# A hybrid attention and MLP step on one core: new tables for the order of loads, splits and joins around a ring of 53 tiles

## The chip, the cores and the metric

The kernel runs on one core of one Trainium2 chip. The metric is the device time of one execution in microseconds; the times given are medians of several runs. Engines are named as in the profile: PE (TensorE, with PEld for its weight loads), DVE (VectorE), ACT (ScalarE), POOL (GpSimd) and SP (SyncE, here only the issuer of transfers).

## The reference, cut to what matters

Two streams of 128 tokens (`prompt` and `sample`, width 2048) go through one layer with the same weights, in float32:

```
shift1, scale1, gate1, shift2, scale2, gate2 = split(silu(c) @ w_ada + b_ada, 6)
h  = rms_norm(x, norm1_w) * (1 + scale1) + shift1
qA, kA, vA, qB, kB, vB, gA, gB = split(h @ w_in)          # 2048 x 8704
oA = windowed GQA (8 heads, 2 key heads, sink), oB = neighbourhood attention (8 heads)
     # sample queries also see cached context keys
x  = x + gate1 * ((sigmoid(gA) * (oA @ w_br_a) + sigmoid(gB) * (oB @ w_br_b)) @ w_out)
h2 = rms_norm(x, norm2_w) * (1 + scale2) + shift2
y  = x + gate2 * (relu(h2 @ w_up) ** 2 @ w_down)          # 2048 x 8192 and back
```

The outputs are `y` of both streams and the new keys and values of the prompt.

## The kernel before, in words

**Products.** Each float32 product is made of three products of fp32r halves: high by high, low by high, high by low. A weight tile `raw` (128x1024, 512 KB) is loaded by SP (L243); ACT copies its high half `wH` (`copy`, L112; `prep_hi`); DVE subtracts to get the low half `wL` (`prep`, L272). Then PE does a *step*: 12 matmuls of 128x512, for two k-tiles, two streams and three products (`mm3`, L347 to L349; `start_steps`, L474 to L476 in the in-projection). A few low halves are made by a transfer instead (`minus_plus`, L278, L279: ACT writes minus the high half, and a POOL transfer adds the weight to it); the table `LO_DMA` says which.

**Ring.** All 128x1024 tiles, weights and activations alike, come from one ring of `GEN` = 53 buffers (`G`, L95). A load can only be issued when the buffer that it takes is free.

**Order.** The program is one list of some 460 weight steps. `run` (L314) goes through it once. At step i it emits the loads that are due up to `RUN[i]` steps ahead, the splits (high and low half) up to `LOOK[i]` steps ahead, further high halves up to `AHEAD[i]` steps, then the step's matmuls, and behind them whatever other work is hung at that step: `at(i, ...)` and `ex(i, ...)` for instructions, `load_at(i, ...)` for loads. Nothing is reordered later: each engine and each queue takes its work in the order in which it was emitted. So tables of step numbers set everything.

**Work hung between the steps**, as far as the change and the prediction speak of it:

- *Modulation blocks.* `pair_load` (L356) loads four tiles `araw` of w_ada, and `pair_mm` (L365) puts one block of 16 narrow matmuls (128x256, accumulator `ps_ada`) on PE. `ADA_AT` and `ADA_LD` place those of sub-layer 1 and their loads, `SS_AT` those of the first part of sub-layer 2: six blocks `fb` = 0 to 5, each at the step that the table gives for it. Blocks at the same step follow each other without a weight matmul between them. The other modulation columns are dot products on DVE (`aT`, L1685; `DOTS`, `DOTS1`, `DOTS2` place them).
- *Attention.* `att_job` (L896) makes seven pieces for each of eight items (mixer, stream s, group g); `JOBS` places them. The probabilities must be transposed. Items in `TE` do that on PE: `probs_T` (L964), four 128x128 transposes into the accumulator `ps_PT` (L970), and one ACT copy to `PT`. All other items do it by a transfer: `probs_part` (L973) has ACT write the two 16-bit planes `plPA`, `flip` (L1059) has SP issue a DMA_TRANSPOSE to `pTPA` (L1062), and `join_full` (L1065) has ACT put the planes together as `fTPA`. For an item of the prompt stream (s = 0) the tiles are half as large.
- *Pairs of w_up pieces.* The 16 pieces of w_up go in eight pairs. The first pair is plain; the others go through `up_pair` (L1409), which has eight positions. A position listed in `FAST` is done by seven products of sums instead of eight: two tiles (`x`, `y`), 21 matmuls (L1419 to L1421), and on DVE a *group* of seven operations: `t` (L1506), `XL` (L1510), a sum (L1511), `YB` (L1513), a sum (L1514), `tL` (L1516) and `uL` (L1517). The other positions are plain: two tiles, 24 matmuls, two `wL` on DVE. `XL_DMA` and `YL_DMA` name the positions whose `XL` or `YB` low half is made by a POOL transfer instead (index 8 times pair plus position), and `T_DMA` those whose sums are made early.
- *Down units.* Behind each pair follow four units of w_down; their sums are carried from pair to pair in a ring tile `dsum`. `DS_AWAY` lists those that wait in DRAM instead (`ds`, one 512 KB transfer out and one back each). `AWAY` lists gate tiles that do the same, and `G2_LEAD` says how many steps before the end of a last down unit its gate and its old residual are fetched.

Of the kernel before, what the change touches and what calls it, by code (L numbers as in the profile page):

```python
# [33 lines left out]
SILU_AT = 6  # L34
FB_DVE = 6
FB1 = 14
H_AT = 38
DOTS1 = [20, 27, 30, 34, 34, 34, 38, 42]
# [30 lines left out]
ADA_AT = [None, 5, 14, 16, 22, 34, 40]
XS_AT = {1: 5, 2: 12, 3: 36}  # L70
POST = {('kvA', 0): [66, 70, 73], ('qA', 0): [66, 69, 75, 75, 77], ('qA', 1): [70, 75, 75, 82, 82], ('kB', 0): [75, 77, 79, 80, 82], ('qB', 0): [81, 82, 86, 88, 90], ('kB', 1): [84, 86, 91, 92, 95], ('qB', 1): [85, 92, 99, 100, 100]}
JOBS = [[80, 80, 81, 85, 88, 89, 92], [82, 83, 84, 86, 90, 97, 104], [83, 86, 86, 89, 90, 90, 105], [89, 91, 92, 93, 93, 105, 109], [95, 95, 98, 100, 100, 102, 114], [95, 101, 102, 104, 107, 111, 116], [106, 106, 108, 108, 121, 123, 127], [108, 111, 116, 117, 117, 120, 124]]
# [18 lines left out]
def tile_hybrid_step(ctx: ExitStack, tc: tile.TileContext, a):  # L91
# [143 lines left out]
    def add_step(src, mm, key, half=0, xkey=None, tkey=None):  # L235
# [660 lines left out]
    def att_job(mix, s, g):  # L896
# [512 lines left out]
    def up_pair(p):  # L1409
# [32 lines left out]
        for pos, is_fast in enumerate(kinds):  # L1442
# [37 lines left out]
            def prep_y(b=b, pos=pos):  # L1480
                if "t" in b:
# [378 lines left out]
```

## Time and profile before

| | |
|---|---|
| median of 3 runs | 1313.43 us (1312.73 to 1314.02) |
| the profiled execution | 1312.65 us |
| its span in the profile | 1310.8 us |
| granted TensorE clock | 0.999 of full |
| PE, DVE, ACT, POOL busy | 99%, 86%, 69%, 4% of the span |
| moved by DMA | 400.9 MB, mean 306 GB/s |

The span is the profile's own time from the first to the last recorded event; the execution's time is 1.85 us longer. Busy time is time in which an engine had an instruction under way. Because PE overlaps its matmuls, a row's own duration (0.39 us for a 128x512 matmul) is longer than the distance from one start to the next, and it is the distance that adds up.

### The profile page before, as it was taken

To read this page: it belongs to the slowest core of one execution; us is meant where nothing else is said; L and a number is where in the kernel's file an instruction comes from. 1 tells how busy PE (TensorE), PEld (TensorE's weight loads), DVE (VectorE), ACT (ScalarE), POOL (GpSimd) and SP (SyncE) were. 2 spreads that over 40 slices of the span, in tenths; PEclk is the share of its full clock that TensorE was granted. 3 is DMA by queue.
4 is the path that set the end of the run, shared out by engine and by line. 5 is a ranking of instruction groups with operands and counts; after the bars stand their busy time and mean duration, and the time that the engine had idled before them with its cause. 6 is when DMAs were issued, how large, how long until landed. Compare 5 with 4: busy or idle time off the path is not lost.

```text
span 1310.8 us, 17957 instructions
## 1 busy us (share of the span) xinstructions
PE 1303.2 (99%) x6333; PEld 1057.9 (81%) x6334; DVE 1126.5 (86%) x1446; ACT 904.5 (69%) x1145; POOL 57.4 (4%) x66
## 2 busy tenths in 40 slices
PE   9999999999999999999999999999999999999998
PEld 4778788788788878888888888888888888888887
DVE  4669799989999899999778998987999998789663
ACT  5635566699865655636786878859779597696980
POOL 0000000332000000000000000000000000000000
PEclk9999999999999999999999999999999999999999
DMA  9999999897999989997599789779977978869593
GB/s 371 408 409 408 400 409 389 346 321 232 271 347 349 386 294 365 359 334 235 205 300 318 204 269 287 275 269 273 322 240 238 362 245 278 301 205 367 193 355 96
DMA packets 170138, 400.90 MB, mean 306 GB/s; under 512 B 71840, under 2 KB 73088, under 8 KB 170048
## 3 DMA queue, kind: packets, MB, share of 16 engines
q1 hardware_dynamic: 165744, 387.36, 82.3%
q0 software_dynamic: 4160, 12.32, 5.0%
q8 instruction: 49, 0.80, 0.2%
q14 instruction: 41, 0.34, 0.1%
q10 hardware_dynamic: 144, 0.08, 0.1%
HBM read 373.97 MB, written 10.80 MB: 294 GB/s over the span
## 4 chain that ended last, share of the span: by engine, by line
PE 98%; ACT 1%; DMA 1%; SPq 0%; issue 0%; DVE 0%; ACTq 0%
PE acc L347 17%; PE acc L348 17%; PE acc L349 17%; PE Q L1421 6%; PE Q L1420 6%; PE Q L1419 6%; PE acc L474 5%; PE acc L475 5%; PE acc L476 5%; PE ps_ada L365 3%; PE ps_S L920 1%; PE Z L1421 1%; PE Z L1420 1%; PE Z L1419 1%; DMA araw<-in_w_pair 1%; PE acc L1225 1%
## 5 line engine op out<-in xcount | busy, mean ns | idle before, releaser
L272 DVE TENSOR_TENSOR wL<-raw,wH 128x1024 fp32r<-128x1024 f32 x377 | 442.7, 1219 | 51.2 <-ACT wH L112 49.0
L112 ACT ACTIVATE wH<-raw 128x1024 fp32r<-128x1024 f32 (+1 forms) x394 | 388.5, 1039 | 62.3 <-DMA raw<-in_w_in 22.6
L474 PE MATMUL acc<-wH,hH 128*128 128x512 f32 x272 | 107.1, 394 | 0.6 <-ACT srow L112 0.6
L475 PE MATMUL acc<-wL,hH 128*128 128x512 f32 x272 | 105.9, 389 | 0.0
L476 PE MATMUL acc<-wH,hL 128*128 128x512 f32 x272 | 105.9, 389 | 0.0
L347 PE MATMUL acc<-wH,hH 128*128 128x512 f32 x252 | 101.2, 402 | 0.0
L348 PE MATMUL acc<-wL,hH 128*128 128x512 f32 x252 | 98.3, 390 | 0.0
L349 PE MATMUL acc<-wH,hL 128*128 128x512 f32 x252 | 98.2, 390 | 0.0
L1685 DVE CUSTOM_DVE_ANT_0 aT<-aT,cB,cols 128x1024 f32<-128x1024 f32 x56 | 71.4, 1283 | 0.6
L1685 DVE CUSTOM_DVE_ANT_0 junk<-aT,cB,cols 128x1024 bf16<-128x1024 f32 x56 | 71.2, 1279 | 0.0
L112 ACT ACTIVATE uH<-raw 128x1024 fp32r<-128x1024 f32 x34 | 36.1, 1062 | 47.4 <-DVE raw L1514 38.2
L474 PEld LDWEIGHTS acc<-wH,hH 128*128 128x128 f32 x272 | 51.0, 188 | 14.2 <-issue 2.9
L476 PEld LDWEIGHTS acc<-wH,hL 128*128 128x128 f32 x272 | 51.1, 188 | 10.8
L475 PEld LDWEIGHTS acc<-wL,hH 128*128 128x128 f32 x272 | 51.1, 188 | 10.2
L347 PEld LDWEIGHTS acc<-wH,hH 128*128 128x128 f32 x252 | 47.4, 188 | 10.6 <-issue 1.0
L348 PEld LDWEIGHTS acc<-wL,hH 128*128 128x128 f32 x252 | 47.4, 188 | 10.5 <-issue 0.7
L349 PEld LDWEIGHTS acc<-wH,hL 128*128 128x128 f32 x252 | 47.3, 188 | 9.9
L112 ACT ACTIVATE tH<-t 128x1024 fp32r<-128x1024 f32 x31 | 32.8, 1058 | 30.4 <-DVE t L1506 26.2
L112 ACT ACTIVATE fTa<-pTa 128x2048 uint16<-128x2048 uint16 x16 | 40.5, 2533 | 1.3 <-DVE gc_g L1685 1.3
L1685 DVE CUSTOM_DVE_ANT_0 aT<-aT,cB,gc_g 128x1024 f32<-128x1024 f32 x32 | 40.7, 1282 | 0.4
L1685 DVE CUSTOM_DVE_ANT_0 junk<-aT,cB,gc_g 128x1024 bf16<-128x1024 f32 x32 | 40.7, 1280 | 0.0
L1562 ACT ACTIVATE up<-up 128x1024 f32<-128x1024 f32 x28 | 29.7, 1062 | 15.4 <-DVE up L1552 14.9
(694 smaller groups left out, 3351.9 us busy)
## 6 DMA issues: line engine op xcount, KB each, us to landing
raw<-in_w_in SPq DMA_DIRECT2D x131, 512.0 KB, 9.0
raw<-in_w_down SPq DMA_DIRECT2D x128, 512.0 KB, 6.8
araw<-in_w_pair SPq DMA_DIRECT2D x80, 512.0 KB, 9.8
raw<-in_w_upF SPq DMA_DIRECT2D x68, 512.0 KB, 6.3
aT<-in_w_gT SPq DMA_DIRECT2D x64, 512.0 KB, 7.1
raw<-in_w_up SPq DMA_DIRECT2D x60, 512.0 KB, 6.8
aT<-in_w_adaT SPq DMA_DIRECT2D x48, 512.0 KB, 8.0
raw<-in_w_out SPq DMA_DIRECT2D x32, 512.0 KB, 7.8
```

The lines of the kernel that those rows point to most:

```text
L112: act.activation(out, in_, AF.Copy)
L272: dve.tensor_tensor(st["lo"], st["raw"], st["hi"].bitcast(F32), op=OP.subtract)
L347: pe.matmul(acc[tb], sh, wh[:, k, :], start=f, stop=False, **kw)
L348: pe.matmul(acc[tb], sh, wl[:, k, :], start=False, stop=False, **kw)
L349: pe.matmul(acc[tb], sl, wh[:, k, :], start=False, stop=l, **kw)
L474: pe.matmul(acc[tb], sh, wh[:, k, :], start=kt == 0 and k == 0 and not held and not seeded, stop=False, **kw)
L475: pe.matmul(acc[tb], sh, wl[:, k, :], start=False, stop=False, **kw)
L476: pe.matmul(acc[tb], sl, wh[:, k, :], start=False, stop=last and k == 1 and not hold, **kw)
L1419: pe.matmul(acc, stat[0], hi, start=f, stop=False)
L1420: pe.matmul(acc, stat[0], lo, start=False, stop=False)
L1421: pe.matmul(acc, stat[1], hi, start=False, stop=l)
L1685: dve.tensor_tensor_reduce(out, box["raw"], cB[s, tag], 1.0, dst if second else baT[:, part, fb:fb + 1], OP.mult, OP.add, dst)
```

## The change

Only tables change; the functions are the same. In the new tables:

- `SS_AT` puts the six modulation blocks of sub-layer 2 at steps 49, 73 (three) and 140 (two) instead of 53 (two), 73 (two), 125 and 141.
- `TE` no longer lists item ('A', 0, 1): its probabilities go by a transfer.
- `FAST` has seven-product groups at other positions in pairs 1, 2, 4, 5 and 7; the number in each pair is the same. Pair 7 now has three in a row (2, 3, 4).
- `XL_DMA` now makes 6 `XL` by transfer instead of 10, `YL_DMA` 8 `YB` instead of 7, `LO_DMA` 11 low halves instead of 7.
- `DS_AWAY` parks 5 down sums instead of 8; `AWAY` parks one gate instead of two.
- `G2_LEAD` fetches the last gates and residuals three steps later, and `ADA_LD` the modulation tiles of sub-layer 1 up to three steps earlier.
- `LOOK`, `RUN`, `AHEAD` and the tables that place the other work (`DOTS`, `POST`, `JOBS`, `T_PAIR`, `P_PAIR` and more) are new throughout.

```
-H_AT = 38
...
+H_AT = 26
...
-TE = (('A', 0, 1), ('qA', 1), ('qB', 1))
-DS_AWAY = [8, 9, 12, 15, 19, 21, 22, 23]
+TE = (('qA', 1), ('qB', 1))
+DS_AWAY = [16, 19, 21, 22, 23]
 DS_BACK = 6
-YL_DMA = [8, 9, 15, 23, 29, 31, 39]
-T_DMA = {15: 10, 48: 10, 55: 7}
+YL_DMA = [8, 9, 15, 16, 23, 29, 31, 63]
+T_DMA = {15: 10, 48: 11, 55: 7}
 G2_PARTS = 1
 PREP_LATE = 9
-G2_LEAD = 2
-ADA_LD = [1, 1, 0, 2, 0, 0, 0]
+G2_LEAD = -1
+ADA_LD = [2, 1, 3, 2, 0, 0, 0]
 BEGIN_SEED = ()
-FAST = {1: (0, 1, 5, 7), 2: (0, 2, 3, 5, 7), 3: (0, 2, 3, 5, 7), 4: (0, 1, 3, 6, 7), 5: (0, 1, 3, 5, 7), 6: (0, 1, 3, 5, 7), 7: (0, 1, 3, 5, 7)}
-AWAY = [('gB', 0), ('gB', 3)]
-GATE_BACK = 3
...
+FAST = {1: (0, 1, 3, 7), 2: (0, 2, 4, 5, 7), 3: (0, 2, 3, 5, 7), 4: (0, 1, 3, 5, 7), 5: (0, 1, 3, 4, 7), 6: (0, 1, 3, 5, 7), 7: (0, 2, 3, 4, 7)}
+AWAY = [('gB', 3)]
+GATE_BACK = 0
...
-LO_DMA = {186: 8, 205: 8, 218: 9, 357: 6, 402: 6, 448: 7, 455: 3}
...
+LO_DMA = {157: 10, 184: 10, 204: 8, 285: 8, 320: 7, 328: 7, 350: 3, 351: 7, 402: 10, 452: 10, 454: 5}
...
-XL_DMA = {9: 8, 16: 10, 21: 7, 23: 9, 26: 7, 35: 9, 38: 11, 43: 9, 55: 10, 61: 8}
...
+XL_DMA = {9: 8, 16: 8, 19: 5, 21: 7, 23: 9, 38: 10, 43: 9, 55: 10, 61: 10, 62: 9}
...
-SS_AT = [53, 53, 73, 73, 125, 141]
+SS_AT = [49, 73, 73, 73, 140, 140]
```

(An index in `XL_DMA` that stands at a plain position has no effect.) Three places show how the order moves. In the rows below, numbers behind a name are those of a buffer's use and differ between the two programs.

**PE, in the products with w_br_a and w_br_b.** `acc` is a weight unit's accumulator; `ps_ada<-araw,cpad` is a modulation block. The trace counts two records to each of its matmuls, so x16 here is x32 in the rows of the trace. Before, the last two blocks of `SS_AT` stood apart, in two places:

```order
L348 MATMUL acc<-wL,hH_1159 128x512
L349 MATMUL acc<-wH,hL_1160 128x512
L365 MATMUL ps_ada<-araw,cpad 32x256 x16
L347 MATMUL acc<-wH,hH_1698 128x512
L348 MATMUL acc<-wL,hH_1698 128x512
...
L348 MATMUL acc<-wL,oHB_3839 128x512
L349 MATMUL acc<-wH,oLB_3840 128x512
L365 MATMUL ps_ada<-araw,cpad 32x256 x16
L347 MATMUL acc<-wH,oHB_4147 128x512
L348 MATMUL acc<-wL,oHB_4147 128x512
```

Now:

```order
L348 MATMUL acc<-wL,oHB_3883 128x512
L349 MATMUL acc<-wH,oLB_3884 128x512
L365 MATMUL ps_ada<-araw,cpad 32x256 x32
L347 MATMUL acc<-wH,oHB_3883 128x512
L348 MATMUL acc<-wL,oHB_3883 128x512
```

The two are one block of 32. Of the other four, which were 32 and 32 in two places, one now stands alone earlier (16) and three together (48). In all there are nine blocks behind the first 47 us where there were ten.

**ACT, in the attention stage**, around the item that leaves PE. `plPA` and `fTPA` are the item's planes and their join, `PT` the copy of what PE transposed, `plqB`, `fTqB` and `plkB` those of other tiles. Before:

```order
L112 ACTIVATE wH<-raw 128x1024 x3
L112 ACTIVATE fTPA_3120<-pTPA_3090 128x2x512
L112 ACTIVATE wH<-raw 128x1024 x2
L112 ACTIVATE fTqB_3153<-pTqB_3088 128x2x1024
L857 ACTIVATE fTqB_3153<-fTqB_3153,cols 128x1024
L112 ACTIVATE PT<-ps_PT 128x512
L112 ACTIVATE plkB_3195<-u_kB_2300 128x1024 x2
```

Now:

```order
L112 ACTIVATE wH<-raw 128x1024
L112 ACTIVATE fTPA_3120<-pTPA_3031 128x2x512
L112 ACTIVATE plPA_3122<-prob 128x512 x2
L112 ACTIVATE wH<-raw 128x1024 x4
L112 ACTIVATE fTqB_3154<-pTqB_3118 128x2x1024
L857 ACTIVATE fTqB_3154<-fTqB_3154,cols 128x1024
L112 ACTIVATE fTPA_3161<-pTPA_3159 128x2x512
L945 ACTIVATE prob,den<-ps_S,nm 128x256 x4
L951 ACTIVATE es<-es 128x4
L112 ACTIVATE plkB_3207<-u_kB_2335 128x1024 x2
```

`PT` is gone; two `plPA` and one `fTPA` have come. On SP the item's transpose is the fourth in a row, ahead of the next weight load; before, three stood there.

**DVE, in pair 7 of w_up**, from the end of one group on. Before, two `wL` of a plain position stood between groups:

```order
L1516 TENSOR_TENSOR tL<-t_10815,tH 128x1024
L1517 TENSOR_TENSOR uL<-raw,uH 128x1024
L272 TENSOR_TENSOR wL<-raw,wH 128x1024 x2
L1506 TENSOR_TENSOR t_10898<-raw 128x1024
L1511 TENSOR_TENSOR raw<-t_10898,raw 128x512
```

Now three groups follow each other:

```order
L1516 TENSOR_TENSOR tL<-t_10729,tH 128x1024
L1517 TENSOR_TENSOR uL<-raw,uH 128x1024
L1506 TENSOR_TENSOR t_10760<-raw 128x1024
L1510 TENSOR_TENSOR XL<-raw,XH 128x1024
L1511 TENSOR_TENSOR raw<-t_10760,raw 128x512
L1513 TENSOR_TENSOR YB<-raw,YB 128x512
L1514 TENSOR_TENSOR raw<-raw 128x512
L1516 TENSOR_TENSOR tL<-t_10760,tH 128x1024
L1517 TENSOR_TENSOR uL<-raw,uH 128x1024
L1506 TENSOR_TENSOR t_10805<-raw 128x1024
```

The third group is full, with its `XL` on DVE; a block of four `wL` stands behind it.

## Rows read from the trace of the kernel before

**Rows 1.** The page, part 1: busy time and share of the span, instructions.

```profile
PE 1303.2 (99%) x6333; PEld 1057.9 (81%) x6334; DVE 1126.5 (86%) x1446; ACT 904.5 (69%) x1145; POOL 57.4 (4%) x66
```

**Rows 2.** The page, part 4: the chain that ended last, by engine.

```profile
PE 98%; ACT 1%; DMA 1%; SPq 0%; issue 0%; DVE 0%; ACTq 0%
```

**Rows 3.** Waits of PE: line waited for, us in total, times, longest.

```profile
PE ps_warm L136 <- DVE wm L129: 1.2, 1, 1.2
```

**Rows 4.** Timeline of PE at 308 us: start, us, engine, line, tiles, shapes.

```profile
308.31 0.39 PE L349 MATMUL acc<-wH,hL 128*128 128x512 f32 x1
...
309.67 0.39 PE L349 MATMUL acc<-wH,hL 128*128 128x512 f32 x1
309.90 0.60 PE L970 MATMUL ps_PT<-ident,prob 128*128 128x128 f32 x4
...
310.80 0.40 PE L349 MATMUL acc<-wH,hL 128*128 128x512 f32 x1
```

**Rows 5.** Timeline of PE at 194 us: a joined block.

```profile
194.04 0.39 PE L476 MATMUL acc<-wH,hL 128*128 128x512 f32 x1
194.36 3.66 PE L365 MATMUL ps_ada<-araw,cpad 128*32 128x256 f32 x64
...
198.52 0.39 PE L476 MATMUL acc<-wH,hL 128*128 128x512 f32 x1
```

**Rows 6.** Timeline of PE at 421 us: a block that stands alone.

```profile
421.50 0.39 PE L349 MATMUL acc<-wH,hL 128*128 128x512 f32 x1
421.82 1.93 PE L365 MATMUL ps_ada<-araw,cpad 128*32 128x256 f32 x32
...
424.26 0.39 PE L349 MATMUL acc<-wH,hL 128*128 128x512 f32 x1
```

**Rows 7.** Timeline of PE at 268 us.

```profile
268.03 0.39 PE L347 MATMUL acc<-wH,hH 128*128 128x512 f32 x1
...
268.62 0.39 PE L349 MATMUL acc<-wH,hL 128*128 128x512 f32 x1
```

**Rows 8.** Timeline of DVE at 267 us.

```profile
267.03 3.48 DVE L272 TENSOR_TENSOR wL<-raw,wH 128x1024 fp32r<-128x1024 f32 x3
```

**Rows 9.** Windows: us, busy PE, PEld, DVE, ACT, POOL, clock, DMA share, GB/s.

```profile
30.00:60.00 30.00, 29.36 (x180) 22.75 (x179) 20.55 (x28) 21.09 (x33) 0.00 (x0) 1.00 1.03 408
300.00:330.00 30.00, 30.00 (x154) 25.21 (x153) 27.16 (x42) 28.92 (x51) 3.66 (x3) 1.00 0.76 199
1170.00:1200.00 30.00, 30.00 (x135) 24.82 (x134) 29.25 (x30) 21.57 (x28) 0.87 (x1) 1.00 0.89 316
```

**Rows 10.** Timeline of ACT, 294 to 320 us: pieces of attention items.

```profile
296.21 1.15 ACT L112 ACTIVATE plPA<-prob 128x512 uint16<-128x512 uint16 x2
...
311.02 1.40 ACT L112 ACTIVATE fTPA<-pTPA 128x1024 uint16<-128x1024 uint16 x1
...
317.78 0.58 ACT L112 ACTIVATE PT<-ps_PT 128x512 f32<-128x512 f32 x1
```

**Rows 11.** Timeline of SP's queue at 302 us: transposes.

```profile
302.31 12.55 SPq L1062 DMA_TRANSPOSE pTPA<-plPA  x2
```

**Rows 12.** Timeline of DVE, 1170 to 1181 us: a group, start to start.

```profile
1170.32 1.23 DVE L116 TENSOR_TENSOR a13L<-fTa,a13H 128x1024 fp32r<-128x1024 f32 x1 [3.72 <-ACT a13H L112]
1171.46 2.35 DVE L272 TENSOR_TENSOR wL<-raw,wH 128x1024 fp32r<-128x1024 f32 x2
1173.73 1.22 DVE L1506 TENSOR_TENSOR t<-raw 128x1024 f32<-128x1024 f32 x1
...
1180.29 1.22 DVE L1506 TENSOR_TENSOR t<-raw 128x1024 f32<-128x1024 f32 x1
```

**Rows 13.** Timeline of PE at 1179 us: the first product of pair 7.

```profile
1179.36 0.39 PE L1419 MATMUL Q<-XH,h20H 128*128 128x512 f32 x1
```

**Rows 14.** Timeline of PE at 71 us: behind a modulation block.

```profile
71.32 0.50 PE L474 MATMUL acc<-wH,hH 128*128 128x512 f32 x1
```

**Rows 15.** Timeline of SP's queue at 1286 us.

```profile
1286.28 0.34 SPq L1583 DMA_DIRECT2D out_y_prompt<-x1b  x1
```

More of the change, by code (lines that the diff above doesn't have):

```diff
@@ L36 @@
 FB1 = 14
-H_AT = 38
-DOTS1 = [20, 27, 30, 34, 34, 34, 38, 42]
+H_AT = 26
+DOTS1 = [18, 28, 31, 34, 34, 35, 38, 42]
 CHUNKS = [2, 2, 2, 4, 6]
@@ L56 @@
-AWAY = [('gB', 0), ('gB', 3)]
-GATE_BACK = 3
-SEED_IN = {3: -1, 4: -1}
+FAST = {1: (0, 1, 3, 7), 2: (0, 2, 4, 5, 7), 3: (0, 2, 3, 5, 7), 4: (0, 1, 3, 5, 7), 5: (0, 1, 3, 4, 7), 6: (0, 1, 3, 5, 7), 7: (0, 2, 3, 4, 7)}
+AWAY = [('gB', 3)]
+GATE_BACK = 0
+SEED_IN = {3: -1, 4: 0}
 SEED_AT = 4
 DIRECT = (3,)
-LO_DMA = {186: 8, 205: 8, 218: 9, 357: 6, 402: 6, 448: 7, 455: 3}
-LOOK = "320000020500002000113432224544355446105343223385524450433655335345220455511216541254444406744443240165443463136211143544456397555524342453545433224531546677753453557412434789853455586466303567898461134235331776545653214545433434534422123768733734502102522243854523655760005645555536452367642004332333245620031043144643220323340312252125324443413423321411333333446345833326123111223423654523544524557100124130023323212212653354124352222546524348984222137443"
@@ L66 @@
-CONST_AT = [73, 75]
-XL_DMA = {9: 8, 16: 10, 21: 7, 23: 9, 26: 7, 35: 9, 38: 11, 43: 9, 55: 10, 61: 8}
+LO_DMA = {157: 10, 184: 10, 204: 8, 285: 8, 320: 7, 328: 7, 350: 3, 351: 7, 402: 10, 452: 10, 454: 5}
+LOOK = "321120021500113212223432223344442225005343223375534342423655446345220456622316541254444404744443240065433351036222042434453289545523232344667633114531546677653453557645534688853485586468513567897361134235333996534653214524222446767643234766513734512102532243864523655860003644655325231155424223132323346742242243144542222302340312252126324443413423322633442234456355833327123111223422543623544502557200224130023545242212653354110142222546412236685233237443"
@@ new lines @@
+RUN = "878887888999967489774426566652243043332113515655542236844445543454663225725104564635347113386421231025420310432200023642333255530101233552468375724663533896686664869999999999799967677624674845057865762774435787755674676471011155366289975888700001010012023644555422226413232357543567947344664412222454243314331337774655600562333412455543455532421531552123100023944336934475787876510000441302144625845546341022443004889667656654243123677999787767425666774210"
+AHEAD = "221111000000000000000000000000000000000000122113121111111211101011122221001010133110000100000333100021133111112211133200001011244001000000000111001111010000000000000010111000111000000000121244220100020000000002320000000003022411110111110002000002111345442330002136444661455741000000000011000003100000002220000000000000000120000010000000001000200111223363222222000000000010000020000000013322222200011112223422222123000202100001100200013121123545251212345402"
@@ L68 @@
+CONST_AT = [66, 71]
+XL_DMA = {9: 8, 16: 8, 19: 5, 21: 7, 23: 9, 38: 10, 43: 9, 55: 10, 61: 10, 62: 9}
 ADA_G = ((1,), (2,), (3, 4), (5, 6))
[L69 to L72, printed above, removed]
+ADA_AT = [None, 5, 14, 16, 22, 35, 40]
@@ new lines @@
+XS_AT = {1: 3, 2: 14, 3: 40}
+POST = {('kvA', 0): [66, 70, 73], ('qA', 0): [64, 69, 74, 76, 78], ('qA', 1): [70, 75, 75, 82, 82], ('kB', 0): [73, 77, 79, 81, 83], ('qB', 0): [78, 82, 86, 89, 90], ('kB', 1): [84, 86, 91, 93, 98], ('qB', 1): [86, 97, 98, 100, 100]}
+JOBS = [[80, 80, 83, 85, 86, 89, 93], [82, 83, 84, 86, 90, 94, 106], [83, 86, 86, 89, 90, 90, 103], [86, 90, 92, 93, 93, 105, 109], [94, 94, 101, 102, 102, 106, 116], [96, 103, 104, 106, 109, 109, 115], [106, 107, 108, 108, 118, 122, 127], [109, 111, 114, 117, 119, 122, 126]]
@@ L73 @@
 SS_G = [(0, 2), (2, 1)]
-SS_AT = [53, 53, 73, 73, 125, 141]
+SS_AT = [49, 73, 73, 73, 140, 140]
 T_AT = [3, 4]
-PREP_IN = [4, 7]
-DOTS = [37, 45, 46, 50, 50, 51, 52, 54, 56, 56, 56, 57, 61, 63, 65, 67, 70, 73, 77, 84, 89, 91, 92, 93, 96, 97, 102, 103, 104, 106, 108, 109, 109, 112, 114, 117, 118, 120, 122, 122, 123, 126, 129, 129, 129, 132, 133, 137, 138, 138, 140, 144, 145, 146, 156, 156, 156, 160, 160, 163, 167, 169, 173, 173, 175, 175, 178, 179, 179, 182, 182, 183]
-DOTS2 = [225, 231, 234, 235, 237, 238, 245, 245, 258, 266, 268, 270, 270, 294, 300, 301, 306, 327, 328, 331, 333, 336, 349, 359, 360, 362, 363, 367, 394, 395, 396, 401]
@@ L79 @@
-STAT_AT = [2, -1, 9, 1]
-T_PAIR = [[14, 4], [6, 9], [8, 8], [5, 8], [8, 9], [5, 10], [6, 12]]
-P_PAIR = [[5, -1], [1, 1], [0, 5], [1, 5], [1, 6], [0, 5], [3, 0]]
+PREP_IN = [6, 7]
+DOTS = [30, 46, 49, 50, 50, 52, 54, 54, 56, 56, 56, 56, 57, 62, 64, 67, 70, 73, 77, 84, 89, 91, 92, 93, 96, 97, 102, 103, 104, 106, 108, 109, 109, 112, 114, 117, 118, 120, 122, 122, 123, 126, 129, 129, 129, 132, 133, 137, 138, 138, 140, 144, 145, 148, 155, 156, 157, 160, 161, 163, 167, 169, 173, 173, 175, 175, 178, 179, 179, 182, 183, 188]
@@ L82 @@
+DOTS2 = [222, 231, 233, 234, 237, 238, 245, 245, 264, 266, 268, 270, 270, 291, 300, 301, 304, 327, 328, 331, 333, 336, 349, 359, 360, 362, 363, 367, 392, 395, 396, 401]
+STAT_AT = [6, 2, 9, 11]
+T_PAIR = [[14, 4], [5, 9], [10, 8], [5, 8], [9, 7], [8, 10], [12, 12]]
+P_PAIR = [[5, -1], [1, 2], [1, 4], [2, 3], [0, 2], [4, 5], [2, 1]]
 M_TE = (3,)
-M_AT = [1, 2, 6]
+M_AT = [1, 2, 8]
 FLIP = 1
-P_UP = [4, 2]
-T_UP = [13, 11]
+P_UP = [5, 3]
+T_UP = [13, 10]
 COL = {"qA": 0, "kvA": 1024, "qB": 1536, "kB": 2560, "vB": 3584, "gA": 4608, "gB": 6656}
```

2 lines of the change are left out of this document (removed).

## The prediction

> **What bounds the kernel now.** I read four views, in this order. The page's busy times say that PE has an instruction under way for 1303.2 of 1310.8 us [rows 1]; only 7.6 us of the span are left. The chain that ended last says the same from the other side: 98% of it is PE, nothing else has more than 1% [rows 2]. So the time is the sum of what stands in PE's queue, unless something makes PE wait. The view of PE's waits has five entries; the largest is 1.2 us [rows 3], and all five belong to the start, before weight products run without a break. Last I read PE's timeline for the distance from one weight matmul to the next: from 308.31 to 309.67 there are six, 1.36 / 6 = 0.227 us each [rows 4]. A row's own 0.39 us is overlapped and may not be added up. A step of 12 matmuls is thus 2.72 us.
>
> DVE at 86% and ACT at 69% [rows 1] are off the path on average, but not everywhere: ACT is busy for 28.92 of 30 us in the attention stage from 300 us, DVE for 29.25 of 30 in w_up's last pair from 1170 us [rows 9]. There a change of order can turn into a wait of PE.
>
> The profiled execution took 1312.65 us, 0.78 below the median of 1313.43. I form the sum against the execution and carry the difference over to the median.
>
> **The change part by part.**
>
> *The attention item that leaves PE.* Its four transposes stand in PE's queue between two weight matmuls whose starts are 1.13 us apart (309.67 to 310.80), with three weight distances in that stretch: 1.13 - 0.68 = 0.45 us [rows 4]. This goes: **-0.45 us**. In exchange ACT makes two plane copies (1.15 together) and a join (1.40) and saves a copy (0.58): +1.97 us [rows 10], where it has 1.08 us idle in 30 [rows 9]. SP gets a fourth transpose in a row; two of them, with their waits, held its queue for 12.55 us [rows 11], so one more is worth 0 to 6.3 us to the loads behind it. Neither is on the path as long as splits and loads are ahead of PE. The new tables let loads be issued up to eight steps (22 us) and splits four (11 us) ahead there. I take 0 and keep +1.97 us, the whole ACT time, as the upper end.
>
> *The joined modulation blocks.* A block of 32 (x64 in the trace's count) stretches the distance around it from 3 x 0.227 = 0.68 to 4.48 us: it costs 3.80 [rows 5]. One of 16 (x32) costs 2.76 - 0.68 = 2.08 [rows 6]. Two apart are 4.16, together 3.80; each separate block costs 0.36 us for its being separate. PE's order has nine blocks behind the first 47 us and had ten: **-0.36 us**. The block of 48 and the single one of 16 are priced by the same split of 1.72 us per 16 matmuls plus 0.36, so only the count of blocks matters. Bounds: 0 if the fixed part is that of neighbours that stay, 0.72 if two joins count.
>
> *A small hitch at 268 us.* Two starts that should be 0.45 us apart are 0.59 apart [rows 7]: PE's low-half product waited for the first `wL` of three, which began at 267.03 behind a block of DVE work on a query tile and ended 1.2 us later [rows 8]. In the new order that `wL` stands ahead of the query's work. **-0.14 us**, with 0 as the other end.
>
> *Seven-product groups in other places.* The number of groups is the same, so PE has the same weight matmuls (5382 in both orders). What moves is DVE's work. A group takes 1180.29 - 1173.73 = 6.56 us on DVE [rows 12], while PE needs 21 x 0.227 = 4.77 us for it: DVE falls back 1.79 us per group. A plain position is 2.27 us on DVE (1171.46 to 1173.73) against 24 x 0.227 = 5.45 on PE: DVE gains 3.18. Pair 7 now has three groups in a row, all with `XL` on DVE. I lay them out from the row at 1170.32: group 0 begins at 1173.73 and ends at 1180.29; two `wL` end at 1182.56; the groups at positions 2, 3 and 4 begin at 1182.56, 1189.12 and 1195.68. The last one's `tL` ends one `uL` earlier than the group (1.14): 1201.10. PE starts the pair at 1179.36 [rows 13] and reaches the first product with that `tL` after 21 + 24 + 21 + 21 + 6 + 4 = 97 matmuls: 1179.36 + 97 x 0.227 = 1201.38. That is **0.3 us in time**. I take 0; the other end is the slower rival.
>
> *Low halves moved between DVE and transfers.* Four more `XL` on DVE and one fewer `YB`, two fewer `wL`: about +2 us of DVE in 1310, and -2 us of ACT's negated copies. Away from pair 7 this is covered by DVE's 14% of idle time; I take 0, and without that cover it is counted in pair 7 already.
>
> *Fewer parked tiles, other loads.* Three down sums and a gate no longer go out and back: eight transfers of 512 KB less. At the full rate of 408 GB/s such a tile takes 1.285 us [rows 9], but PE waits for no load behind the start, so it gains 0. In the first 60 us the transfers are the scarce thing (share 1.03, [rows 9]). There the modulation tiles of f = 2 now pass weight tiles. In SP's new order 46 tiles of 512 KB go out up to the weights of step 17: 46 x 1.285 = 59.1 us, some 62 with the start. The first product behind the block at that place begins at 71.32 [rows 14]. 9 us in hand; 0, at the other end about 1 us if splits queue up too. At the end, the last gate and residual are now fetched behind the output at 1286.28 [rows 15], some 13 us before the last unit's first half needs them, ten times a tile's 1.285 us: 0.
>
> **Sum:** -0.45 - 0.36 - 0.14 = **-0.95 us**. The profiled execution would take 1311.7, the median 1313.43 - 0.95 = **1312.5 us**. That is 0.07%, below the 0.2% (2.6 us) which a measurement of this kernel can tell from no change.
>
> [...] The trace shows the four transposes at 0.45 us of PE and their replacement at 1.97 us of ACT plus a transfer. [...]
>
> **The rivals.**
>
> 1. *ACT runs out of lead in the attention stage.* Place: 300 to 330 us. For it: ACT is busy for 28.92 of 30 us there. Against it: PE waited for no high half in that stretch before, although ACT was as full. Price: up to the whole 1.97 us, so 1312.5 + 1.97 = 1314.5.
> 2. *The join does not do what it says.* The words speak of two joins, but the order has only one block less, and the other regrouping splits one pair to make a three. If a block's fixed price lies in work that stays, or small hitches of that size come up elsewhere, only the transposes count: 1313.43 - 0.45 = 1313.0.
> 3. *Slower: DVE misses pair 7.* One mechanism: three groups in a row with no `XL` by transfer. Its margin by the rows is 0.3 us, and its start hangs on an ACT copy for which DVE had idled 3.72 us [rows 12]. Each us beyond the margin is a us of PE, since nothing later gives PE idle time back. The upper price is the fall-back of all three, 3 x 1.79 = 5.4 us: 1312.5 + 5.4 = 1317.9. It decides the sign by the 0.2% when DVE starts the pair 3.9 us later than in the trace (0.3 of margin, then 2.63 + 0.95 of wait). Against it: DVE's idle 3.72 us lie just ahead of the pair, so a part of them is a cushion if the copy comes sooner.
> 4. *Faster by over 0.2%.* Even with all five waits of the start gone, the 7.6 us outside PE's busy time are mostly warm-up, first loads and the tail, which the tables don't touch. I find no place for 2.6 us.
>
> **How the numbers follow.** Forecast 0.62 (1311.6 to 1313.2 by its own bounds); rival 1 has 0.15, rival 2 0.11, rival 3 0.08 and rival 4 0.04. Rivals 1 and 2 lie within 0.2% of 1313.43, so *same* has 0.62 + 0.15 + 0.11 = 0.88, *slower* 0.08, *faster* 0.04. The range: down by the second join's 0.36 and the spread of runs below the median (0.70) from 1312.5, 1311.4; up to rival 1's 1314.5 and the spread above (0.59), 1315.0 rounded. Rivals 3 and 4 are left out, 12 in 100.
>
> **What would show it.** In the changed profile: rows of L970 gone; a x64 block in the merge products and a x96 one earlier, with distances of about 4.5 and 6.2 us around them; PE's weight distance still 0.227; PE's busy time and the span about 1 us lower; PE's waits still those of the start. Rival 1 would show as distances over 0.23 us at high-half products (L347, L474) between 300 and 340 us; rival 3 as a gap of PE ahead of an L1420 with `tL` near 1200 us, behind DVE that has no idle time from 1170 on. The forecast is wrong if the span moves by more than 2 us, or if the time moves by 1 us in rows that I priced at nothing.

## The result, and the profile after

| | before | the change |
|---|---|---|
| median of the runs | 1313.36 us (7 runs, 1312.48 to 1314.02) | 1316.50 us (7 runs, 1315.75 to 1318.93) |
| ratio | | 1.0030 (95%: 1.0019 to 1.0042) |
| profiled execution, its span | 1312.65, 1310.8 us | 1315.75, 1314.0 us |

The change made the kernel slower by 3.1 us where 0.95 us less had been forecast, and its executions spread over 3.2 us, those of the kernel before over 1.5. The page's busy times and chain of the changed kernel, which answer to [rows 1, 2]:

```profile
PE 1302.9 (99%) x6330; PEld 1057.4 (80%) x6330; DVE 1129.1 (86%) x1447; ACT 906.1 (69%) x1147; POOL 56.4 (4%) x65
...
PE 96%; DMA 3%; ACT 1%; SPq 0%; issue 0%; DVE 0%; ACTq 0%
```

PE is busy for 0.3 us less, but the span is 3.2 us longer: what came is waiting, and the chain says for what. DMA has 3% of it, three times as much as before. The view of PE's waits names the tile:

```profile
PE ps_ada L365 <- DMA araw<-in_w_pair: 3.1, 4, 1.0
```

This line is new; the next largest wait is that of [rows 3]. PE waits four times for tiles of modulation weights. PE's timeline shows where; first the one at the start, in the changed kernel, and then the other three, inside the joined block of 48 matmuls (x96 in the trace's count, here in pieces x72, x8, x8 and x8):

```profile
20.37 0.64 PE L365 MATMUL ps_ada<-araw,cpad 128*32 128x256 f32 x8 [0.99 <-DMA araw<-in_w_pair]
...
251.86 4.09 PE L365 MATMUL ps_ada<-araw,cpad 128*32 128x256 f32 x72
256.47 0.64 PE L365 MATMUL ps_ada<-araw,cpad 128*32 128x256 f32 x8 [0.52 <-DMA araw<-in_w_pair]
257.75 0.64 PE L365 MATMUL ps_ada<-araw,cpad 128*32 128x256 f32 x8 [0.64 <-DMA araw<-in_w_pair]
259.39 0.64 PE L365 MATMUL ps_ada<-araw,cpad 128*32 128x256 f32 x8 [1.00 <-DMA araw<-in_w_pair]
259.96 0.66 PE L869 MATMUL ps_qT<-ident,u_kvA 128*128 128x128 f32 x4
```

The three pieces of x8 are 1.3 to 1.6 us apart. That is about the pace of the transfers (1.285 us for 512 KB at 408 GB/s, [rows 9]), not of PE, which does a piece in 0.43 us (1.72 us per 16 matmuls). From the block's first start to that of `ps_qT` it takes 8.10 us. A block of 32 at this place takes 3.59 us (253.67 to 257.26 in the trace of e2 below), and 16 matmuls more are 1.72: 5.31. (In e4 below, where the same block of 48 doesn't wait, it takes 5.32.) So **2.79 us are waiting**. The bracketed idle times add up to less (2.16), because each row's own 0.64 us overlaps. SP's queue in the same trace says why the tiles are late:

```profile
234.17 14.40 SPq L356 DMA_DIRECT2D araw<-in_w_pair  x12
```

And in the kernel before:

```profile
234.10 8.49 SPq L356 DMA_DIRECT2D araw<-in_w_pair  x8
```

The burst of modulation tiles begins at the same time in both, but it has twelve tiles instead of eight. Twelve take 14.40 us to issue, at the full rate of the transfers, and the last lands 10.8 us after its issue (248.57 to 259.39). The burst did not begin sooner because SP was held up at the loads that stand ahead of it in its queue: between 200 and 230 us it waits once for 7.9 us until PE (L476) and once for 3.8 us until DVE (L272) has used a tile, that is, for free ring buffers. The windows of the changed kernel show it as transfers that stand idle (the columns are those of [rows 9]):

```profile
200.00:230.00 30.00, 30.00 (x134) 24.83 (x133) 29.96 (x45) 20.16 (x29) 0.00 (x0) 1.00 0.71 263
230.00:260.00 30.00, 27.85 (x194) 20.59 (x192) 28.97 (x43) 14.49 (x25) 19.05 (x17) 1.00 1.03 410
```

First 263 GB/s, then 410 and no more to be had. But waits for buffers are only a part of the idle time. From 216.3 to 218.5 us SP issues five small loads of constants (`rope` with 128 KB, three `cpad` with 64 KB each, `sink` with 4 KB), and while these are under way the transfers crawl; `sink` with its 4 KB takes 8.9 us from issue to landing. Loads of 512 KB had been issued behind them by then (`cbv`, at 220.05, takes 10.2 us to land). In the kernel before the same five stand shortly ahead of the burst. First a window of the changed kernel, then one of the kernel before:

```profile
218.00:227.00 9.00, 9.00 (x41) 7.48 (x40) 8.96 (x13) 6.87 (x11) 0.00 (x0) 1.00 0.44 132
```

```profile
234.00:238.00 4.00, 4.00 (x20) 3.30 (x19) 2.19 (x4) 2.93 (x7) 1.22 (x2) 1.00 0.09 26
```

So it seems that loads which are next to nothing in bytes held up the burst too. No run moved them, so their share in the wait is not shown. Two smaller things add to it. On ACT a high half that waits 7.44 us for one of the weight tiles behind the burst stands ahead of `S`, the copy of the block's result:

```profile
260.95 1.06 ACT L112 ACTIVATE wH<-raw 128x1024 fp32r<-128x1024 f32 x1 [7.44 <-DMA raw<-in_w_in]
261.92 1.07 ACT L112 ACTIVATE u_vB<-acc 128x512 f32<-128x512 f32 x2
262.87 0.60 ACT L112 ACTIVATE S<-ps_ada 128x512 f32<-128x512 f32 x1
```

PE's selection matmuls wait for `S` (from the weight matmul ahead of them to the one behind it is 0.93 us, in the kernel before 0.59: 0.34 more). The other is the wait at 20 us, 1.0 us. Both programs issue the same transfers in the same order up to there, and the runs below show that it differs from execution to execution: in the three traces of the changed kernel alone the first in-projection product of L474 begins at 37.05, 36.31 and 36.41 us, in all fourteen traces of this study between 35.95 and 37.13. To leave this out I compare from that product to PE's last one. Before, and then in the changed kernel:

```profile
36.05 0.47 PE L474 MATMUL acc<-wH,hH 128*128 128x512 f32 x1 [0.65 <-ACT srow L112]
...
1306.56 0.28 PE L1361 MATMUL acc<-wH,a15L 128*128 128x256 f32 x1
```

```profile
37.05 0.47 PE L474 MATMUL acc<-wH,hH 128*128 128x512 f32 x1 [0.65 <-ACT srow L112]
...
1309.68 0.28 PE L1361 MATMUL acc<-wH,a15L 128*128 128x256 f32 x1
```

That is 1270.51 and 1272.63: the **main part** of the changed kernel is 2.12 us longer in this execution. The forecast of -0.95 and the two delays of 2.79 and 0.34 give +2.18.

### The profile page after: what moved, and what is told of

The parts are those of the page before. It is cut to its first block, busy times and chain, and to the rows that moved or that the text cites. A ratio compares the mean times of both kernels' runs of the same rounds, so it can differ in the third digit from the quotient of the medians.

```text
span 1314.0 us, 17950 instructions
## 1 busy us (share of the span) xinstructions
PE 1302.9 (99%) x6330; PEld 1057.4 (80%) x6330; DVE 1129.1 (86%) x1447; ACT 906.1 (69%) x1147; POOL 56.4 (4%) x65
## 4 chain that ended last, share of the span: by engine, by line
PE 96%; DMA 3%; ACT 1%; SPq 0%; issue 0%; DVE 0%; ACTq 0%
PE acc L347 17%; PE acc L349 17%; PE acc L348 17%; PE Q L1419 6%; PE Q L1421 6%; PE Q L1420 6%; PE acc L474 5%; PE acc L476 4%; PE acc L475 4%; PE ps_ada L365 2%; DMA araw<-in_w_pair 2%; DMA raw<-in_w_in 1%; PE ps_S L920 1%; PE Z L1419 1%; PE Z L1421 1%; PE Z L1420 1%
## 5 line engine op out<-in xcount | busy, mean ns | idle before, releaser
L272 DVE TENSOR_TENSOR wL<-raw,wH 128x1024 fp32r<-128x1024 f32 x375 | 441.5, 1223 | 40.7 <-ACT wH L112 39.9
L474 PE MATMUL acc<-wH,hH 128*128 128x512 f32 x272 | 107.1, 394 | 0.6 <-ACT srow L112 0.6
L476 PE MATMUL acc<-wH,hL 128*128 128x512 f32 x272 | 105.9, 389 | 0.0
L474 PEld LDWEIGHTS acc<-wH,hH 128*128 128x128 f32 x272 | 51.1, 188 | 14.2 <-issue 2.1
L476 PEld LDWEIGHTS acc<-wH,hL 128*128 128x128 f32 x272 | 51.1, 188 | 10.7
L112 ACT ACTIVATE dsum<-acc 128x512 f32<-128x512 f32 x56 | 31.2, 588 | 20.5 <-PE acc L349 19.7
L365 PE MATMUL ps_ada<-araw,cpad 128*32 128x256 f32 x640 | 38.7, 382 | 3.3 <-DMA araw<-in_w_pair 3.1
L1506 DVE TENSOR_TENSOR t<-raw 128x1024 f32<-128x1024 f32 x31 | 37.9, 1221 | 3.8 <-DMA raw<-in_w_upF 1.7
## 6 DMA issues: line engine op xcount, KB each, us to landing
araw<-in_w_pair SPq DMA_DIRECT2D x80, 512.0 KB, 10.2
```

What stands on the lines that cost most here:

```text
L112: act.activation(out, in_, AF.Copy)
L272: dve.tensor_tensor(st["lo"], st["raw"], st["hi"].bitcast(F32), op=OP.subtract)
L474: pe.matmul(acc[tb], sh, wh[:, k, :], start=kt == 0 and k == 0 and not held and not seeded, stop=False, **kw)
L476: pe.matmul(acc[tb], sl, wh[:, k, :], start=False, stop=last and k == 1 and not hold, **kw)
```

## The experiments

The main part is the distance just defined, in the profiled execution; before: 1270.51. The wait is that inside the block at 252 us, by its distance.

| run | modulation blocks (matmuls) | median, us | ratio to before (95%) | main part | wait |
|---|---|---|---|---|---|
| the change | 16, 48, 32 | 1316.50 | 1.0030 (1.0019 to 1.0042) | 1272.63 | 2.79 |
| e1, the same | 16, 48, 32 | 1317.09 | 1.0028 (1.0019 to 1.0037) | 1272.35 | 2.30 |
| e2 | 32, 32, 32 | 1312.34 | 0.9994 (0.9985 to 1.0002) | 1269.49 | 0 |
| e3, before | 16, 48, 16, 16 | 1316.48 | 1.0024 (1.0016 to 1.0033) | 1271.89 | 1.50 |
| e4 | 16, 48, 32 | 1322.01 | 1.0065 (1.0052 to 1.0078) | 1278.48 | 0 |
| e5 | 16, 32, 16, 32 | 1314.80 | 1.0012 (1.0003 to 1.0021) | 1272.53 | 0 in the first, 2.0 in the next |
| e6 | 16, 48, 32 | 1321.15 | 1.0059 (1.0045 to 1.0073) | 1279.17 | see below |
| e7, before | 32, 32, 16, 16 | 1312.94 | 0.9999 (0.9990 to 1.0007) | 1270.51 | 0 |
| e8, before | 32, 32, 32 | 1312.68 | 0.9997 (0.9988 to 1.0006) | 1270.16 | 0 |
| e9 | 32, 32, 32 | 1312.77 | 0.9996 (0.9987 to 1.0005) | 1270.32 | 0 |
| e10, e2 again | 32, 32, 32 | 1312.52 | 0.9994 (0.9985 to 1.0002) | 1269.73 | 0.14 |

**e1: the changed kernel again.** No edit.

> The changed kernel once more, to see which of its waits are there in every execution. Theory A (the late burst): PE's wait inside the block of 48 at about 252 us comes from the twelve modulation tiles whose transfers are issued in one burst from 234 us; it is in the program and comes back, 2 to 3.5 us. The other new wait, 1.0 us ahead of a modulation block at 20 us, stands where both programs issue the same transfers in the same order: theory A expects it to differ from execution to execution, so this trace may lack it and the span then be about 1313.0. Rival B (the whole stretch is short of transfers from the start on): both waits come back, the span is 1314.0 again.

The wait inside the block came back (2.30 us), and so did that for `S` (0.57 by the distance used above). The wait at the start was shorter: the first product of L474 begins at 36.31 instead of 37.05, and the span is 1312.9. So the first two are in the program, and the start is chance. But the median of the eleven executions is 1317.09 with a spread from 1314.71 to 1318.64, and the profiled one is the fastest of all, as it was in the first trace. Why most are slower is asked in e11.

**e2: the second block back to an earlier step.**

```
-SS_AT = [49, 73, 73, 73, 140, 140]
+SS_AT = [49, 49, 73, 73, 140, 140]
```

> The changed kernel with one number changed back in kind: the second of the six modulation blocks of sub-layer 2 goes from step 73 to step 49, so that blocks of 32, 32 and 32 stand where 16, 48 and 32 stood. PE's work and the count of separate blocks stay the same; only four of the twelve tiles leave the burst. Theory A: PE's waits inside the block at 252 us go, and the time falls by 2.5 to 3.5 us against the changed kernel, to 1312.8 to 1314.0, at or below the kernel before. Rival B (the burst is only where a shortage shows that SP's earlier stops on the ring made): the wait moves to the next tiles, weights or modulation, and less than 1 us is won.

One number, and the time falls by 4.2 us against the change's first median, to just below the kernel before (by the times alone the two are the same, the interval of the ratio reaches 1.0002) and 0.5 us below theory A's range. In its trace the burst is of eight and PE doesn't wait:

```profile
237.12 9.29 SPq L356 DMA_DIRECT2D araw<-in_w_pair  x8
```

```profile
253.67 3.66 PE L365 MATMUL ps_ada<-araw,cpad 128*32 128x256 f32 x64
257.26 0.66 PE L869 MATMUL ps_qT<-ident,u_kvA 128*128 128x128 f32 x4
```

The last tile of the eight is out by 246.4 and the block runs through from 253.67 to its end. It is in time by little: in e10, the same kernel, the block takes 3.73 us instead of 3.59. The main part is 1.02 us shorter than before. All eleven executions lie between 1311.62 and 1312.70.

**e3: the block of 48 in the kernel before.**

```
-SS_AT = [53, 53, 73, 73, 125, 141]
+SS_AT = [53, 73, 73, 73, 125, 141]
```

> The kernel before with that one move alone: the second modulation block goes from step 53 to step 73, so 16, 48, 16 and 16. PE's work and the count of separate blocks stay as before. Theory A: the burst of twelve tiles appears and PE waits inside the block at 252 us; in the kernel before the eight tiles were issued from 234.1 us, so twelve end about 5 us later than eight did, and the wait is 1.5 to 4 us: 1315 to 1317.5. Rival B (it takes the new tables' stops of SP between 199 and 230 us): no wait, 1313.4 as before.

The wait comes with that one move, without any of the other tables: 1.50 us in the profiled execution, and a median 3.2 us above before. The spread comes with it too (1313.72 to 1318.92). So it doesn't take the new order's stops of SP; in e3's three windows of 10 us from 200 on the transfers had 284, 385 and 349 GB/s, well over the 263 of the change, and twelve tiles were too many all the same. What this doesn't show is that twelve are too many for transfers that run at the full rate throughout: in e3 the small loads stand shortly ahead of the burst, as in the kernel before, and from 230 to 240 us the transfers moved 197 GB/s (200 in the kernel before).

**e4 and e6: the loads earlier.** Both move SP's issues of the six blocks' tiles ahead, by four steps (shown) and by two (`i - 2`):

```
-                load_at(i, lambda box=box, fb=fb: pair_load(box, 1, fb))
+                load_at(i - 4, lambda box=box, fb=fb: pair_load(box, 1, fb))
```

> The changed kernel with the loads of the six blocks of sub-layer 2 moved four steps ahead in SP's order (past three to five weight loads each); the blocks themselves stay at their places. Theory A: the twelve tiles land 3 to 5 us sooner and the wait inside the block falls by most of its 2.8 us; the weight loads that they pass come 5 to 15 us later, which their splits can partly take: 1313 to 1315. Rival B: what is won at the block is lost at the weights behind it, 1316 or more, with new waits of PE on high or low halves between 235 and 300 us.

> The changed kernel with the loads of the six blocks two steps ahead in SP's order instead of four; the burst of twelve passes two weight loads. Theory A: the tiles land 2.6 us sooner, the wait inside the block falls to 0 to 0.5 us, but the two weight tiles that were passed land behind twelve others, 15 us later; four steps gave one wait of 7.2 us, two steps less of lateness for those weights, about 2 x 2.7 us, leaves 1 to 3 us: 1313.5 to 1316. If the passed weights have slack enough: 1312.3.

e4 came out on rival B's side, at a higher price; e6 is 5 us above its expectation. With four steps the block itself no longer waits, but the weights that the burst passed hold PE up once for 7.2 us. With two steps there is still a wait in the block, and the high half of a passed weight blocks ACT for 8.93 us. The normalised key tile stands behind it on ACT (L826) and DVE, and PE's transposes of that tile wait:

```profile
257.57 0.64 PE L365 MATMUL ps_ada<-araw,cpad 128*32 128x256 f32 x8 [0.72 <-DMA araw<-in_w_pair]
262.41 0.55 PE L869 MATMUL ps_qT<-ident,u_kvA 128*128 128x128 f32 x2 [4.21 <-DVE u_kvA L829]
263.74 0.66 PE L869 MATMUL ps_qT<-ident,u_kvA 128*128 128x128 f32 x2 [0.77 <-DVE u_kvA L839]
```

And the wait is not all. Windows of e6 show that TensorE's granted clock falls to 0.50 behind it:

```profile
255.00:262.00 7.00, 2.49 (x44) 1.01 (x36) 0.16 (x1) 2.89 (x5) 0.00 (x0) 1.00 0.97 386
...
264.00:266.00 2.00, 2.00 (x7) 1.61 (x6) 2.00 (x3) 2.00 (x6) 1.14 (x1) 0.50 0.84 250
```

From 264 to 269 us weight products follow each other every 0.427 us instead of 0.227 (the clock is 0.50 in both windows from 264 to 268 us); from 270 us on it is at 1.00 again. The same happens in e4: its granted clock is 0.50 from 256 to 258 us, behind the 7.2 us, and its main part is 8.99 us over e2's, 1.8 more than the wait. So at none of the three places tried in SP's order (as in the change, two steps and four steps ahead) do twelve tiles go in one piece: at the end of the stretch the modulation tiles are late, further ahead the weights are.

**e5: the third block one step later.**

```
-SS_AT = [49, 73, 73, 73, 140, 140]
+SS_AT = [49, 73, 73, 74, 140, 140]
```

> The changed kernel with the third block of the 48 one step later (step 74), so 16, 32, 16 and 32: one separate block more (0.36 us), and its four tiles are due one step and the end of the block later, 2.7 us or more, while they stand behind one more weight load (1.3 us). Theory A (the join itself is right, the deadline of the last tiles is what costs): PE's wait shrinks from 2.8 to 0 to 1.5 us, time 1312.3 + 0.36 + 0 to 1.5 = 1312.7 to 1314.2, with a smaller spread than the changed kernel's. Rival B' (a bigger share comes from the weights that the burst holds up, not from the block): the wait stays above 2 us and shows at weight products or at the selection matmuls behind the block, 1315 or more.

1314.80 is 0.6 us above what theory A allowed. The first block of 32 runs through, but the third's last two tiles are late again, by 1.1 and 0.9 us:

```profile
258.26 1.07 PE L365 MATMUL ps_ada<-araw,cpad 128*32 128x256 f32 x16
260.26 0.64 PE L365 MATMUL ps_ada<-araw,cpad 128*32 128x256 f32 x8 [0.92 <-DMA araw<-in_w_pair]
261.54 0.64 PE L365 MATMUL ps_ada<-araw,cpad 128*32 128x256 f32 x8 [0.64 <-DMA araw<-in_w_pair]
```

```profile
234.41 9.19 SPq L356 DMA_DIRECT2D araw<-in_w_pair  x8
246.04 0.33 SPq L243 DMA_DIRECT2D raw<-in_w_in  x1
249.02 1.94 SPq L356 DMA_DIRECT2D araw<-in_w_pair  x4
```

PE's demand moved back by a step, but so did SP's issue of the last four tiles: it stands still from 243.6 to 246.0 and from 246.4 to 249.0 us, and in the change the twelfth was out by 248.6. I had counted one weight tile of 1.3 us between them and not the two stops. The profile puts the first stop (2.3 us) down to PE's products at L476 and the second (2.6 us) to DVE's work on `u_qA` (L839), which fits ring buffers that come free. The main part is 3.04 us over e2's: 0.36 for the separate block, 2.0 of waiting, and the rest, some 0.7, mostly at attention scores between 277 and 288 us (`ps_S`, which waits once for ACT).

**e7: the attention item alone, in the kernel before.**

```
-TE = (('A', 0, 1), ('qA', 1), ('qB', 1))
+TE = (('qA', 1), ('qB', 1))
```

> The kernel before with the one attention item moved from PE to a transfer, nothing else. PE theory (the forecast's): the four transposes' 0.45 to 0.49 us go from PE's queue and nothing waits: span 1310.3, time 1312.8. ACT theory (rival 1 of the prediction): ACT's 1.97 us more show as waits of PE between 300 and 340 us, 1313.3 to 1315.

Both theories had a part. The transposes are gone from PE at 310 us, but a wait for a low half that was not there before stretches the next two distances at 336 from 0.227 to 0.58 and 0.34 us and so costs 0.47:

```profile
335.17 0.39 PE L347 MATMUL acc<-wH,hH 128*128 128x512 f32 x1
335.75 0.50 PE L348 MATMUL acc<-wL,hH 128*128 128x512 f32 x1 [0.19 <-DVE wL L272]
336.09 0.40 PE L349 MATMUL acc<-wH,hL 128*128 128x512 f32 x1
```

The chain behind it is rival 1's. ACT copies the output of an attention item (`oHA`) 1.63 us later than before (324.88 against 323.25), for the planes and the join stand ahead of it; DVE's subtraction waits for that copy (first the kernel before, then e7); and the three `wL` behind it begin at 334.48 instead of 332.79.

```profile
323.88 0.69 DVE L1000 TENSOR_TENSOR oLA<-ps_o,oHA 128x512 fp32r<-128x512 f32 x1 [0.59 <-ACT oHA L112]
```

```profile
325.50 0.69 DVE L1000 TENSOR_TENSOR oLA<-ps_o,oHA 128x512 fp32r<-128x512 f32 x1 [1.84 <-ACT oHA L112]
```

The main part is the same as before, 1270.51: the 0.45 us that were won are given back.

**e8: the last two blocks joined, in the kernel before.**

```
-SS_AT = [53, 53, 73, 73, 125, 141]
+SS_AT = [53, 53, 73, 73, 141, 141]
```

> The kernel before with its last two modulation blocks joined (steps 141 and 141 instead of 125 and 141), nothing else. Theory A: this join has eight tiles in a row but a stretch with transfers to spare, so only the fixed price of one block goes, 0.36 us: the distance around the joined block is 4.5 us and the time 1312.9, with no wait on a modulation tile. Rival (every join makes a burst that PE waits for): a wait of 1 us or more inside the block, 1314 or more.

The main part is 0.35 us shorter, without a wait inside the block: what the forecast gave for the join, 0.36. A join of eight tiles is cheap to load at that place.

**e9 and e10: the item back on PE, in the kernel of e2; and e2 again, without an edit.**

```
-TE = (('qA', 1), ('qB', 1))
+TE = (('A', 0, 1), ('qA', 1), ('qB', 1))
```

> The kernel of e2 (second modulation block at step 49) with the attention item's four transposes put back on PE. PE theory: 0.45 to 0.49 us more than e2's kernel, as the four transposes' distance said, so about 1312.8. Rival (as in e7, where a wait of PE for a low half at 336 us gave most of it back): the new tables have the same kind of hitch somewhere, and the two kernels differ by less than 0.2 us in PE's timeline from the first in-projection product to the end.

> The kernel of e2 once more, beside e9 on the same chip and against the kernel before. If the forecast's sum (0.95 us) was right but for the burst, its PE timeline from the first in-projection product to the end is again 0.8 to 1.1 us shorter than in the kernel before, the time 1312.2 to 1312.6, and all its executions lie within about 1.5 us, as those of e2 did and those of the changed kernel did not.

e10's main part is 0.78 us shorter than before (e2's was 1.02), e9's 0.19. Not all of the 0.59 to 0.83 us between e9 and the two traces of e2's kernel belongs to the item. In e9's trace its transposes stand here:

```profile
310.21 0.39 PE L349 MATMUL acc<-wH,hL 128*128 128x512 f32 x1
310.44 0.60 PE L970 MATMUL ps_PT<-ident,prob 128*128 128x128 f32 x4
...
311.34 0.40 PE L349 MATMUL acc<-wH,hL 128*128 128x512 f32 x1
```

That is 1.13 us with three weight distances in it, so 0.45 us for the transposes, as before the change. Behind 311 us the timelines differ by no more than 0.05 us further, so in the new tables nothing is given back. The other 0.1 to 0.4 us arose ahead of the item, mostly at the key transposes and the modulation block near 257 us, where two traces of one kernel (e2 and e10) differ by 0.2 us. The medians, 1312.77 against 1312.52, point the same way, but on their own they couldn't tell it.

**e11 and e12: the change and e3 once more, one profiled execution each.**

> The changed kernel a third time, one look: its executions spread over 4 us (1314.7 to 1318.9) where the others spread over 1 us, and both traces so far are of its fastest ones. If the spread comes from how late the burst's last tiles land, this trace's wait inside the block at 252 us makes up the difference of its time to e2's kernel (1312.3), whatever that is; if something else spreads, its time is over 1316 with a wait under 3 us. If a long wait also lets TensorE's clock fall, as in e6, distances of 0.43 us follow the block.

> The kernel of e3 (the kernel before with the block of 48) a second time, one look, for the same question: its executions spread from 1313.7 to 1318.9 us. The same alternatives as for e11: the wait inside the block accounts for its time over 1312.9 to 1313.3, or it doesn't.

e11 took 1317.64 us, e12 1316.26. In e11 the four last pieces of the block are late, and the products behind it are slow:

```profile
251.22 3.66 PE L365 MATMUL ps_ada<-araw,cpad 128*32 128x256 f32 x64
255.38 0.64 PE L365 MATMUL ps_ada<-araw,cpad 128*32 128x256 f32 x8 [0.50 <-DMA araw<-in_w_pair]
256.89 0.64 PE L365 MATMUL ps_ada<-araw,cpad 128*32 128x256 f32 x8 [0.88 <-DMA araw<-in_w_pair]
258.35 0.64 PE L365 MATMUL ps_ada<-araw,cpad 128*32 128x256 f32 x8 [0.81 <-DMA araw<-in_w_pair]
260.04 0.64 PE L365 MATMUL ps_ada<-araw,cpad 128*32 128x256 f32 x8 [1.05 <-DMA araw<-in_w_pair]
260.61 0.90 PE L869 MATMUL ps_qT<-ident,u_kvA 128*128 128x128 f32 x4
...
262.16 0.63 PE L349 MATMUL acc<-wH,hL 128*128 128x512 f32 x1
262.59 0.63 PE L347 MATMUL acc<-wH,hH 128*128 128x512 f32 x1
```

The wait is 260.61 - 251.22 - 5.31 = 4.08 us, and behind it products are 0.43 us apart until 264.3. The main part is 1275.15, 5.66 us over e2's: 4.08 of waiting, and 1.58 left, which fits the clock (0.72 granted in the mean of 260 to 266 us): some 3 us of products at 0.43 us instead of 0.227. e12 has a wait of 2.82 us, no fall of the clock (1.00 in the same window), and a main part 2.71 us over before. Its start was 0.9 us later than before (36.97 against 36.05), which makes up the rest of its time. So the spread is accounted for in these two: the wait itself differs (1.5 to 4.1 us in five traces of a block of 48), and where it was longest the clock's fall came on top. The slowest executions have no trace, but the record has the granted clock of each. Of the 31 executions of the change and e3 (with e1, e11 and e12), the ten below 1316 us have 0.999 or 1.000, the five above 1318.5 have 0.997, and e11 has 0.999. So the clock fell in the slowest too, and for longer than in e11; how long they waited is not shown.

## Why the prediction was wrong

*What bounds the kernel*: right. In the traced execution of the change, what PE waited and the forecast's own terms give the change of the main part to 0.1 us.

*The attention item*, -0.45: right in the new tables (0.45 by e9), given back in the old ones by a wait for a low half (e7). Rival 1 had the place and the engine right, ACT in the attention stage, but the lateness reached PE by way of DVE, at 0.47 us of the 1.97, and in the old tables only. Where the item was transposed made no difference in the old tables (both main parts are 1270.51), and in the new ones the transfer won 0.45 us; PE was the engine that had no time to spare, busy for 99% of the span.

*The joined blocks*, -0.36: the PE term was right to 0.01 us (e8), and **this is the step that failed**. I priced the blocks by PE alone ("only the count of blocks matters") and asked at neither join, the pair at step 140 or the three at step 73, when the tiles land. For transfers I wrote "PE waits for no load behind the start, so it gains 0". That is true of the kernel before, and it was carried over to a program that asks for twelve tiles at one place where there had been eight. What the runs showed in its place: 2.3 to 4.1 us of waiting in the changed kernel's three traces, 0.3 and 0.6 for `S` in two of them, and 1.6 for the clock in the third. It could have been estimated. The page of the kernel before has the median from issue to landing of such a tile, 9.8 us:

```profile
araw<-in_w_pair SPq DMA_DIRECT2D x80, 512.0 KB, 9.8
```

The burst began at 234.1 us; 12 tiles x 1.285 us end at 249.5; with 9.8 us to land that is 259.3. PE wanted the last tile by 256.7 and began its piece at 259.39. That the sum hits so well is in part luck, for the issue took 14.40 us and the landing 10.8. In the other four traces of a block of 48 the same sum lies between 0.3 us before and 1.7 us after the start of the last piece, good enough to see the wait, not to size it. I had worked it out for the first 60 us, where the transfers looked scarce, and not here, where the order had four tiles more.

*The hitch at 268 us*, -0.14: gone, as forecast, but not changed by itself in any run. The total of 0.78 (e10) to 1.02 us (e2) agrees with the forecast's sum, 0.95.

*Pair 7 and rival 3*: no wait. In e2 the `tL` of the third group ended at 1198.66 and was used at 1201.41, 2.75 us in time where I had 0.3; DVE began the pair sooner, at 1170.43 instead of 1173.73. *Parked tiles, the early loads and the late fetch of the last gate*: no wait in any trace, 0 as taken.

*Rival 2* was wrong: the join did what it says. The slower side did happen, with a mechanism that none of the rivals had.

## What to carry to other kernels

When blocks of work are joined to save a fixed price on the bounding engine, join their loads in the sum as well. Count the tiles that are now due at one place, multiply by the time of one tile at the full rate (1.285 us here), add the time from issue to landing (9.8 us), and compare with the moment of need; look, too, at what stands ahead of them in the queue, for while a few small loads were under way these transfers ran at 26 to 132 GB/s. "The engine has never waited for a load" says nothing of a burst that was not there before. A load pulled ahead in a full queue and a full ring handed its lateness to what it passed (PE waited 7.2 us for it in e4): e2's remedy was to spread the demand, and it won 4.2 us with one number where earlier loads lost 4 to 5 more.

## What the runs showed that I had not expected

The clock behind a wait. After the 4.1 us of waiting in e11, in four pieces with a little PE work between them, the granted clock was 0.72 in the mean of 260 to 266 us, some 3 us of weight products came 0.43 us apart, and that cost 1.6 us; after the waits of 2.79 (the change) and 2.82 (e12) it was 1.00 in the same 6 us. In e6, with 4.21 and 0.77 us close behind a late piece, it was 0.50 from 264 to 268 us and products were slow for 5 us, and in e4 it was 0.50 from 256 to 258 us, with the single wait of 7.2 us. And the first 36 us differ by 0.8 us among the nine traces with the new tables and by 1.0 among the five with the old ones, in which their orders are the same, so gains of a microsecond are read from PE's main part, not from the span.
